# Two buffers for a quarter's output matrices, loaded ahead of its input matrices and transposed one step later

## The chip, the cores and the metric

The kernel runs on one core of a Trainium2 chip. The metric is device time in microseconds (us), and the profile is one execution of the program, recorded by the hardware. Engines are named as the profile does: PE (TensorE matmul), PEld (its weight load), DVE (VectorE), ACT (ScalarE), POOL (GpSimd) and SP (SyncE, which here only issues DMAs). SPq and ACTq are the DMA issues of SP and ACT.

## The reference, cut to what matters

One layer of a decoder trunk, sequence 1024, model width 1024, all float32. A projection makes the inputs of three branches and 3 x 1024 gate logits; the branches are merged under the gates; an output projection, a norm, a SwiGLU block and a second norm follow.

```python
u_s5, x_lru, g_lru, q, k, v, fg, gate_logits = split(x @ w_in)
y_s5  = _s5_branch(u_s5, ...)      # state space, 32 groups x 16 channels, 64 complex states
y_lru = _rglru_branch(x_lru, ...)  # gated linear recurrence, 4 blocks of 128 channels
y_fox = _fox_branch(q, k, v, ...)  # attention with a forget bias, 8 heads
proj  = einsum('blkc,kcd->blkd', stack([y_s5, y_lru, y_fox]), w_branch)
mixed = sum(sigmoid(gate_logits + b_gate) * proj) @ w_out
...
# inside _s5_branch, c = output matrices, b = input matrices of a group
bu = einsum('blgc,gpc->blgp', u, b_bar)
h  = linear_scan(lam_bar, bu)
y  = einsum('blgp,gcp->blgc', h, c).real + d_skip * u
```

## The kernel before, in words

Matmuls reach float32 accuracy in three passes: each operand is split into a high part (ACT casts, `split` at L143) and a low part (DVE subtracts, L129), and `mm3` multiplies high by high, high by low, and low by high. All matmuls of one helper bear L117 in the profile; weights are `wh` and `wl`, activations are two tiles that bear the same letter (`x`, `m` or `s`). A 128 x 512 output from 8 row blocks is 24 matmuls.

Up to the second norm's weights the program is written by three generators that are run against each other: `fox` (attention), `others` (the projection column blocks, `zblock`, 48 matmuls each, and then the merges) and `side` (state space, then the recurrence). Each `yield` adds a number to its generator's clock, and the one with the lowest clock is advanced next; this gives the program order. A scheduler then orders the instructions of each engine by a timeline of its own, with that order as priority, and the result is a fixed, in-order list for each engine. So a number in a `yield` can move instructions on every engine.

`side` first yields 90, then runs `quarter(qd)` for four quarters of 8 groups each (every yield of it times T_S5 = 1.44), then `channel_gate`, then `recurrence` (times T_LRU = 1.246), whose four blocks b = 0 to 3 each do this: a depthwise convolution on DVE; a gate product `ta` and an input product `tx` of 6 matmuls each on PE; tanh on ACT (L844, L845); a reciprocal on DVE (L850); products on POOL; a scan on DVE (L856); a last product on DVE, and a store to `ylru_d` (L859).

`others`, after its last gate block, fetches the four state space outputs and runs `merge(0)`, 16 outputs of 12 matmuls, with L137 on DVE taking each from PSUM; then it fetches the four recurrence outputs back from `ylru_d` (L503) and runs `merge(1)`.

A quarter loads two pairs of input matrices (`b0`, `b1`, L674 and L675) and two natural-layout tiles `nat` of output matrices (L679), transposes each `nat` on PE (L681) and scales it on DVE into `c0` or `c1`. `nat` has one buffer, so the load of the second waits for the transpose of the first. POOL then makes `bb`, `bbs` and the powers `bbp` from the input matrices, and one step later the powers `cl` from the output matrices.

Of the kernel before, what the change touches and what calls it, by code (L numbers as in the profile page):

```python
# [21 lines left out]
P = 128  # L22
# [10 lines left out]
GROUPS, STATES, GCH = 32, 64, 16  # L33
# [24 lines left out]
def trunk(ctx: ExitStack, tc: tile.TileContext, A: dict, out: bass.AP):  # L58
    nc = tc.nc
    PE, ACT, DVE, POOL, SP = nc.tensor, nc.scalar, nc.vector, nc.gpsimd, nc.sync  # L60
# [26 lines left out]
    def name(n):  # L87
        count[0] += 1
        return f"{n}{count[0]}"
# [14 lines left out]
    def few(tag, shape, bufs, pool):  # L104
        return pools[pool].tile(list(shape), F32, name=name(tag), tag=tag, bufs=bufs)
# [4 lines left out]
    def bank(shape=(P, 512), tag="b"):  # L110
        return psum.tile(list(shape), F32, name=name(tag), tag=tag, bufs=3)
# [19 lines left out]
    def ts(e, o, a, s1, op1, s2=None, op2=None):  # L131
        if op2 is None:
            return e.tensor_scalar(o, a, s1, None, op1)
        return e.tensor_scalar(o, a, s1, s2, op1, op2)
# [309 lines left out]
    first_k = done["k"]  # L444


    rows = few("nat", [124, P], 1, "side")

    def put_rows(r, ap, c=slice(0, P)):
        SP.dma_start(rows[r : r + ap.shape[0], c], ap)  # L450
# [213 lines left out]
    c_v = [A["s5_c_re"], A["s5_c_im"]]  # L664
    late_pool = [None]

    def quarter(qd):
        g8 = slice(8 * qd, 8 * qd + 8)
        prm = new("s", shape=(P, 8, 8, GCH))
        b0, b1, c0, c1, bb, bbs = [prm[:, i] for i in range(6)]  # L670
        halves = (slice(0, 64), slice(64, P))
        for i in range(2):
            src = b_v[i][g8].rearrange("g p c -> p g c")
            SP.dma_start(b0[halves[i]], src)  # L674
            SP.dma_start(b1[halves[1 - i]], src)  # L675
        for i, dst in enumerate((c0, c1)):
            nat = few("nat", [P, 2, STATES], 1, "side")
            for e in range(2):
                SP.dma_start(nat[:, e], c_v[e ^ i].rearrange("g c p -> (g c) p")[qd * P : (qd + 1) * P, :])  # L679
            pc = bank([P, 8, GCH])  # L680
            PE.transpose(pc.rearrange("p g c -> p (g c)"), nat.rearrange("p e s -> p (e s)"), ident)  # L681
            ts(DVE, dst, pc, sign, ALU.mult, 1.0 if i == 0 else -1.0, ALU.mult)
# [54 lines left out]
        with after(late_pool[0]):  # L737
            POOL.memset(cc[:, :, 0:1], 1.0)
            POOL.memset(ss[:, :, 0:1], 0.0)
            for i in range(7):  # L740
                n = 1 << i
                e = [t[:, 1 + i, g8].unsqueeze(2).broadcast_to([P, 8, n]) for t in (ctab, stab)]
# [6 lines left out]
        for i in range(2):  # L749
            c = slice(4 * i, 4 * i + 4)  # L750
# [20 lines left out]
        for i in range(2):  # L771
            py = bank([P, 4, P])
            for j in range(4):
                g = 4 * i + j
# [87 lines left out]
    def side():  # L862
        yield T_SIDE
        for qd in range(NB):
            for t in quarter(qd):
                yield T_S5 * t
        yield from channel_gate()
        done["s5"] = True
        for t in recurrence():
            yield T_LRU * t  # L870
        done["lru"] = True
# [277 lines left out]
    for hb in range(NH):  # L1149
        g, more = G[hb], hb + 1 < NH  # L1150
# [199 lines left out]
```

## Time and profile before

| | us |
|---|---|
| median of 3 runs (range) | 1650.58 (1650.56 to 1651.05) |
| the profiled execution's own time | 1650.19 |
| its span, first to last instruction | 1648.4 |
| PE busy in the span | 1592.8 |
| DVE, ACT, POOL busy | 1011.6, 634.5, 599.5 |

The profiled execution's time is its span and 1.8 us around it. PE is busy for 97% of the span, so what can be had or lost is read from PE's idle time, and from the clock that it was granted. A profile row of the timeline names start, duration, engine, line, operation, output and inputs, and in brackets how long the engine was idle before it and what released it.

### The profile page before, as it was taken

What the parts mean: (1) busy time and instruction counts of PE and PEld (TensorE: products, weight loads), DVE (VectorE), ACT (ScalarE), POOL (GpSimd) and SP (SyncE); (2) the same over time, 40 slices, a digit from 0 to 9 for tenths busy, and PEclk for the clock granted to TensorE, in tenths of its full rate; (3) what the DMA queues carried; (4) which work ended last, traced back from release to release, by engine and by line L of the source; (5) the groups of instructions that cost most, each with busy time, mean ns of one, the idle gap of its engine ahead of it and who ended that gap; (6) DMA issues with size and microseconds to landing.
All of it is one profiled execution on the core that took longest, in us unless ns stands there. A gap on an engine that the chain in (4) does not pass through costs nothing.

```text
span 1648.4 us, 20516 instructions
## 1 busy us (share of the span) xinstructions
PE 1592.8 (97%) x7482; PEld 1321.1 (80%) x7482; DVE 1011.6 (61%) x1602; ACT 634.5 (38%) x960; POOL 599.5 (36%) x529
## 2 busy tenths in 40 slices
PE   8989999999899999999999998999999999999997
PEld 6877888877787888888888886788888888778886
DVE  4756575723643467887657769666555555547766
ACT  4425454524633445564213224223222222244442
POOL 0111316333143011112040028599987888400004
PEclk9999999999999999999999998999999999999999
DMA  5343324333332333344754712356544455597752
GB/s 169 76 102 80 80 78 105 77 79 100 88 83 67 116 116 113 114 144 169 246 185 162 244 49 77 126 193 200 171 166 166 154 177 170 202 331 233 245 174 102
DMA packets 219968, 236.09 MB, mean 143 GB/s; under 512 B 33376, under 2 KB 162524, under 8 KB 219868
## 3 DMA queue, kind: packets, MB, share of 16 engines
q1 hardware_dynamic: 192604, 202.83, 39.5%
q10 hardware_dynamic: 27264, 31.96, 5.9%
q8 instruction: 59, 0.97, 0.2%
q14 instruction: 41, 0.34, 0.1%
HBM read 163.96 MB, written 70.78 MB: 142 GB/s over the span
## 4 chain that ended last, share of the span: by engine, by line
PE 78%; DVE 9%; issue 4%; DMA 3%; ACT 3%; POOL 2%; SPq 1%; ACTq 0%; DVEq 0%; POOLq 0%
PE b L117 35%; PE p L117 32%; PE a L117 8%; PE s L117 2%; PE a L341 1%; DMA ws<-w_ffn_down 1%; POOL s L129 1%; DVE r L129 1%; DVE s L129 1%; DVE x L137 1%; DVE wo L129 1%; DMA nck<-ck_d 1%; DVE m L129 1%; DVE x L129 1%; ACT r L1237 1%
## 5 line engine op out<-in xcount | busy, mean ns | idle before, releaser
L117 PE MATMUL b<-x,wh 128*128 128x512 f32 x912 | 351.9, 397 | 2.3 <-ACT s L708 1.7
L117 PE MATMUL b<-x,wl 128*128 128x512 f32 x832 | 328.5, 395 | 0.0
L117 PE MATMUL b<-m,wh 128*128 128x512 f32 x784 | 309.1, 394 | 0.0
L117 PE MATMUL p<-mx,w 128*128 128x512 f32 x1056 | 250.0, 392 | 2.1 <-DVE mx L129 1.3
L117 PEld LDWEIGHTS p<-mx,w 128*128 128x128 f32 x1056 | 199.7, 189 | 44.4 <-issue 1.7
L117 PEld LDWEIGHTS b<-x,wh 128*128 128x128 f32 x912 | 172.9, 190 | 37.4 <-ACT s L708 2.0
L117 PEld LDWEIGHTS b<-x,wl 128*128 128x128 f32 x832 | 157.4, 189 | 31.7
L129 DVE TENSOR_TENSOR x<-x,p 128x512 f32<-128x512 f32 x163 | 108.4, 683 | 109.4 <-PE p L117 92.5
L117 PEld LDWEIGHTS b<-m,wh 128*128 128x128 f32 x784 | 148.8, 190 | 28.7 <-issue 0.2
L117 PE MATMUL p<-w,w 128*128 128x512 f32 x528 | 157.4, 390 | 1.1 <-DVE w L129 1.0
L129 POOL TENSOR_TENSOR s<-s,s 128x1024 f32<-128x1024 f32 (+9 forms) x76 | 77.2, 1015 | 207.4 <-ACT s L852 75.2
L129 DVE TENSOR_TENSOR w<-ws,w 128x1024 fp32r<-128x1024 f32 x88 | 116.0, 1324 | 51.8 <-ACT w L143 51.6
L143 ACT CAST w<-ws 128x1024 fp32r<-128x1024 f32 x88 | 92.1, 1050 | 103.4 <-PE p L117 64.0
L117 PE MATMUL p<-wo,w 128*128 128x512 f32 x528 | 127.3, 389 | 0.0
L129 DVE TENSOR_TENSOR wl<-ws,wh 128x1024 fp32r<-128x1024 f32 x62 | 85.8, 1383 | 65.5 <-ACT wh L143 62.2
L117 PEld LDWEIGHTS p<-w,w 128*128 128x128 f32 x528 | 98.8, 188 | 22.9 <-DVE w L129 2.6
L117 PEld LDWEIGHTS p<-wo,w 128*128 128x128 f32 x528 | 99.1, 188 | 20.5
L143 ACT CAST wh<-ws 128x1024 fp32r<-128x1024 f32 x62 | 65.1, 1050 | 125.0 <-PE b L117 99.2
L129 DVE TENSOR_TENSOR w<-m,w 128x1024 fp32r<-128x1024 f32 x44 | 69.0, 1567 | 63.2 <-ACT w L143 63.2
L129 POOL TENSOR_TENSOR ln<-x,x 128x512 f32<-128x512 f32 x44 | 75.7, 1727 | 63.6 <-ACT x L1172 52.2
L117 PE MATMUL p<-w 128*128 128x512 f32 x264 | 97.5, 390 | 1.1 <-ACT w L143 1.1
L129 POOL TENSOR_TENSOR r<-r,row 128x1024 f32<-128x1024 f32 x7 | 16.7, 2391 | 189.5 <-DVE r L129 184.3
(276 smaller groups left out, 2721.6 us busy)
## 6 DMA issues: line engine op xcount, KB each, us to landing
ws<-w_in SPq DMA_DIRECT2D x48, 512.0 KB, 4.1
ws<-w_ffn_gate SPq DMA_DIRECT2D x27, 512.0 KB, 4.2
gate_d<-zs ACTq DMA_DIRECT2D x48, 256.0 KB, 2.0
zs<-gate_d SPq DMA_DIRECT2D x48, 256.0 KB, 2.8
ws<-w_ffn_up SPq DMA_DIRECT2D x22, 512.0 KB, 4.6
x<-w_ffn_down SPq DMA_DIRECT2D x22, 512.0 KB, 5.6
hid_d<-ln SPq DMA_DIRECT2D x22, 512.0 KB, 3.9
wts_d<-x SPq DMA_DIRECT2D x22, 512.0 KB, 2.6
```

The costliest lines, as they stand in the source:

```text
L117: PE.matmul(o, a, b, start=first, stop=last)
L129: return pin(e.tensor_tensor(o, a, b, op))
L137: return DVE.scalar_tensor_tensor(out=o, in0=a, scalar=s, in1=b, op0=op0, op1=op1)
L143: pin(ACT.copy(hi, src))
L341: PE.transpose(ta[:, j, e, :], pts[e][:, (k0 + j) * P : (k0 + j + 1) * P], ident)
L1237: pin(ACT.activation(r, r, AF.Identity, bias=nm, scale=rs))
```

## The change

The `nat` tag gets two buffers. A quarter issues its four `nat` loads ahead of its four input-matrix loads, yields 5.0 (7.2 on the clock of `side`), and only then transposes. The later steps of a quarter, the channel gate and the recurrence come that much later on the clock of `side`, 28.8 after four quarters.

```diff
--- before.py
+++ after.py
@@ -444,7 +444,7 @@
     first_k = done["k"]
 
 
-    rows = few("nat", [124, P], 1, "side")
+    rows = few("nat", [124, P], 2, "side")
 
     def put_rows(r, ap, c=slice(0, P)):
         SP.dma_start(rows[r : r + ap.shape[0], c], ap)
@@ -669,14 +669,17 @@
         prm = new("s", shape=(P, 8, 8, GCH))
         b0, b1, c0, c1, bb, bbs = [prm[:, i] for i in range(6)]
         halves = (slice(0, 64), slice(64, P))
+        nats = [few("nat", [P, 2, STATES], 2, "side") for _ in range(2)]
+        for i, nat in enumerate(nats):
+            for e in range(2):
+                SP.dma_start(nat[:, e], c_v[e ^ i].rearrange("g c p -> (g c) p")[qd * P : (qd + 1) * P, :])
         for i in range(2):
             src = b_v[i][g8].rearrange("g p c -> p g c")
             SP.dma_start(b0[halves[i]], src)
             SP.dma_start(b1[halves[1 - i]], src)
+        yield 5.0
         for i, dst in enumerate((c0, c1)):
-            nat = few("nat", [P, 2, STATES], 1, "side")
-            for e in range(2):
-                SP.dma_start(nat[:, e], c_v[e ^ i].rearrange("g c p -> (g c) p")[qd * P : (qd + 1) * P, :])
+            nat = nats[i]
             pc = bank([P, 8, GCH])
             PE.transpose(pc.rearrange("p g c -> p (g c)"), nat.rearrange("p e s -> p (e s)"), ident)
             ts(DVE, dst, pc, sign, ALU.mult, 1.0 if i == 0 else -1.0, ALU.mult)
```

**SP's list.** Names are tiles with their numbers; `nat` tiles are the output matrices, `ws` the weights of the projection. Before, at the third quarter, with the next quarter's first tile behind it:

```order
L679 DMA nat688_3519<-s5_c_im 128x64
L679 DMA nat688_3519<-s5_c_re 128x64
L172 DMA ws776_4009<-w_in 128x8x128
L679 DMA nat877_4458<-s5_c_re 128x64
L679 DMA nat877_4458<-s5_c_im 128x64
L172 DMA ws819_4208<-w_in 128x8x128
```

Changed, the third quarter's loads:

```order
L675 DMA nat698_3643<-s5_c_re 128x64
L172 DMA ws665_3323<-w_in 128x8x128
L675 DMA nat698_3643<-s5_c_im 128x64
L675 DMA nat699_3644<-s5_c_im 128x64
L675 DMA nat699_3644<-s5_c_re 128x64
L302 DMA nck568_2815<-ck_d_92 128x8x128
L734 DMA s619_3017<-u_d_522 16x8x128 x8
```

The second tile's loads now follow the first tile's, with no transpose between them, and stand ahead of the quarter's input matrices, which come some ten rows later.

**DVE's list between recurrence block 2 and merge(0).** `s` tiles are the recurrence's, `x` tiles with a `ws` input are the low parts of the state space outputs, `wl` the low parts of the branch weights that merge(0) begins with. Before, from the scan of block 2 on:

```order
L856 SCALAR_TENSOR_TENSOR s1297_6706<-s1306_6739,s1301_6716 128x1024
L129 TENSOR_TENSOR s1297_6706<-s1297_6706,s1296_6703 128x1024
L129 TENSOR_TENSOR s1332_6946<-s1323_6878,s1331_6945 128x1024
L137 SCALAR_TENSOR_TENSOR x1342_6979<-ws1340_6976,x1341_6978 128x1024
L137 SCALAR_TENSOR_TENSOR x1345_6985<-ws1343_6982,x1344_6984 128x1024
L137 SCALAR_TENSOR_TENSOR x1348_6991<-ws1346_6988,x1347_6990 128x1024
L137 SCALAR_TENSOR_TENSOR x1351_6997<-ws1349_6994,x1350_6996 128x1024
L129 TENSOR_TENSOR wl1354_7003<-ws1352_7000,wh1353_7002 128x1024
L129 TENSOR_TENSOR wl1357_7009<-ws1355_7006,wh1356_7008 128x1024
```

Changed, from the reciprocal of block 2 on:

```order
L853 RECIPROCAL s1320_6863<-s1320_6863 128x1024
L137 SCALAR_TENSOR_TENSOR x1330_6939<-ws1328_6936,x1329_6938 128x1024
L137 SCALAR_TENSOR_TENSOR x1333_6945<-ws1331_6942,x1332_6944 128x1024
L134 TENSOR_SCALAR s1358_7042<-s1356_7038,cols91_518 128x1024
L137 SCALAR_TENSOR_TENSOR x1336_6951<-ws1334_6948,x1335_6950 128x1024
L134 TENSOR_SCALAR s1320_6863<-s1320_6863 128x1024
L137 SCALAR_TENSOR_TENSOR s1358_7042<-s1356_7038,cols91_518,s1358_7042 128x1021
L859 SCALAR_TENSOR_TENSOR s1311_6830<-s1320_6863,s1315_6840 128x1024
L137 SCALAR_TENSOR_TENSOR x1339_6957<-ws1337_6954,x1338_6956 128x1024
L137 SCALAR_TENSOR_TENSOR s1358_7042<-s1356_7038,cols91_518,s1358_7042 128x1022
L129 TENSOR_TENSOR s1311_6830<-s1311_6830,s1310_6827 128x1024
L129 TENSOR_TENSOR wl1342_6963<-ws1340_6960,wh1341_6962 128x1024
```

The scan and last product of block 2 stood ahead of all four low parts; now the four stand among them, and the first `wl` of merge(0) stands behind the last product of block 2. On PE's list the last `ta` matmul of block 2 was 156 matmuls ahead of the first one of merge(0) (the 6 of `tx`, three gate blocks of 48, and the 6 `ta` matmuls of block 3); now it is 54 ahead (the 6 of `tx` and one gate block). The first 12 matmuls of merge(0) now all use high parts of weights; the 13th is the first that uses `wl1342`.

**DVE's list between recurrence block 3 and merge(1).** `m` rows take an output of merge(0) from the PSUM tile named last; `wl1418` is the low part of merge(1)'s first weights. Before, around the scan of block 3:

```order
L134 TENSOR_SCALAR s1339_6973<-s1339_6973 128x1024
L137 SCALAR_TENSOR_TENSOR m1371_7092<-zs1372_7093,b1373_7095 128x512
L856 SCALAR_TENSOR_TENSOR s1323_6878<-s1339_6973,s1334_6950 128x1024
L129 TENSOR_TENSOR s1409_7305<-ws1407_7302,s1408_7304 128x1024
L137 SCALAR_TENSOR_TENSOR m1371_7092<-zs1374_7109,a1375_7111 128x512
L129 TENSOR_TENSOR s1323_6878<-s1323_6878,s1322_6875 128x1024
L129 TENSOR_TENSOR s1412_7311<-ws1410_7308,s1411_7310 128x1024
```

Changed:

```order
L137 SCALAR_TENSOR_TENSOR m1389_7189<-zs1390_7190,b1391_7192 128x512
L134 TENSOR_SCALAR s1380_7147<-s1380_7147 128x1024
L137 SCALAR_TENSOR_TENSOR m1389_7189<-zs1392_7206,a1393_7208 128x512
L859 SCALAR_TENSOR_TENSOR s1358_7042<-s1380_7147,s1370_7091 128x1024
L129 TENSOR_TENSOR s1358_7042<-s1358_7042,s1357_7039 128x1024
L129 TENSOR_TENSOR s1412_7311<-ws1410_7308,s1411_7310 128x1024
L137 SCALAR_TENSOR_TENSOR m1394_7230<-zs1395_7231,b1396_7233 128x512
L137 SCALAR_TENSOR_TENSOR m1394_7230<-zs1397_7247,a1398_7249 128x512
L137 SCALAR_TENSOR_TENSOR m1399_7263<-zs1400_7264,b1401_7266 128x512
L137 SCALAR_TENSOR_TENSOR m1399_7263<-zs1402_7280,a1403_7282 128x512
L129 TENSOR_TENSOR s1415_7317<-ws1413_7314,s1414_7316 128x1024
L129 TENSOR_TENSOR wl1418_7323<-ws1416_7320,wh1417_7322 128x1024
```

The scan of block 3 stood behind the output in `b1373`, whose last matmul is 132 ahead of the first of merge(1); now it stands behind the output in `a1393`, whose last matmul is 48 ahead of merge(1). The three instructions that follow on ACT's list are as before: the store of block 3, the cast of its reloaded output, and the cast of merge(1)'s first weights, `wh1417`. On SP the reload and then the loads of those weights follow in this order too.

## Rows read from the trace of the kernel before

**Rows 1.** The page, busy time of each engine in us, its share, instructions.

```profile
PE 1592.8 (97%) x7482; PEld 1321.1 (80%) x7482; DVE 1011.6 (61%) x1602; ACT 634.5 (38%) x960; POOL 599.5 (36%) x529
```

**Rows 2.** Waits of PE: us in total, times, longest.

```profile
PE b L681 <- DMA nat<-s_c_re: 5.1, 3, 2.5
PE a L341 <- DVE pt L133: 3.9, 2, 3.4
```

**Rows 3.** Timeline of PE at the transposes of the third and fourth quarter.

```profile
354.44 0.28 PE L681 MATMUL b<-ident,nat 128*128 128x128 f32 x1
357.06 0.45 PE L681 MATMUL b<-ident,nat 128*128 128x128 f32 x1 [2.35 <-DMA nat<-s_c_re]
...
453.97 0.45 PE L681 MATMUL b<-ident,nat 128*128 128x128 f32 x1 [2.50 <-DMA nat<-s_c_re]
```

**Rows 4.** Timeline of SP: start, duration of the issue.

```profile
355.14 0.42 SPq L679 DMA_DIRECT2D nat<-s_c_re  x1
...
793.97 0.32 SPq L503 DMA_DIRECT2D ws<-ylru_d  x1
794.72 0.93 SPq L172 DMA_DIRECT2D ws<-w_branch  x2
```

**Rows 5.** Stretches behind those transposes; the last three columns: granted clock, DMA share, GB/s.

```profile
357.00:359.00 2.00, 1.95 (x5) 1.60 (x6) 1.96 (x3) 0.00 (x0) 0.00 (x0) 0.50 0.00 0
359.00:361.00 2.00, 2.00 (x8) 1.60 (x7) 0.82 (x2) 0.00 (x0) 1.07 (x1) 0.70 0.83 211
456.00:458.00 2.00, 2.00 (x6) 1.58 (x5) 1.29 (x2) 0.76 (x2) 2.00 (x2) 0.50 0.32 53
458.00:460.00 2.00, 2.00 (x8) 1.57 (x7) 0.00 (x0) 0.00 (x0) 1.92 (x1) 0.70 0.35 99
```

**Rows 6.** Timeline of PE from recurrence block 2 to merge(1).

```profile
730.04 2.58 PE L117 MATMUL b<-s,s 128*128 128x512 f32 x10 [0.53 <-DVE s L129]
...
761.72 0.39 PE L117 MATMUL b<-x,wh 128*128 128x512 f32 x1
...
764.89 0.39 PE L117 MATMUL b<-x,wl 128*128 128x512 f32 x1
...
766.48 1.07 PE L117 MATMUL a<-x,wh 128*128 128x512 f32 x4
...
811.36 0.62 PE L117 MATMUL b<-s,wh 128*128 128x512 f32 x2
```

**Rows 7.** Timeline of DVE from the reciprocal of block 2 to merge(1).

```profile
735.56 6.54 DVE L850 RECIPROCAL s<-s 128x1024 f32<-128x1024 f32 x1
742.03 0.71 DVE L134 TENSOR_SCALAR s<-s,cols 128x1024 f32<-128x1024 f32 x1
742.78 3.31 DVE L137 SCALAR_TENSOR_TENSOR s<-s,cols,s 128x1021 f32<-128x1021 f32 x1
...
750.13 2.28 DVE L856 TENSOR_TENSOR_SCAN s<-s,s 128x1024 f32<-128x1024 f32 x1
752.44 2.36 DVE L129 TENSOR_TENSOR s<-s,s 128x1024 f32<-128x1024 f32 x2
757.23 1.23 DVE L137 SCALAR_TENSOR_TENSOR x<-ws,x 128x1024 fp32r<-128x1024 f32 x1 [2.42 <-ACT x L508]
...
766.52 1.22 DVE L129 TENSOR_TENSOR wl<-ws,wh 128x1024 fp32r<-128x1024 f32 x1
...
789.71 1.22 DVE L129 TENSOR_TENSOR s<-s,s 128x1024 f32<-128x1024 f32 x1
```

**Rows 8.** Timeline of ACT in the same stretch.

```profile
732.56 1.23 ACT L845 ACTIVATE s<-s,c 128x1024 f32<-128x1024 f32 x1
...
790.97 0.33 ACTq L859 DMA_DIRECT2D ylru_d<-s  x1
799.53 1.05 ACT L143 CAST s<-ws 128x1024 fp32r<-128x1024 f32 x1 [8.90 <-DMA ws<-ylru_d]
801.06 1.05 ACT L143 CAST wh<-ws 128x1024 fp32r<-128x1024 f32 x1 [0.48 <-DMA ws<-w_branch]
```

## The prediction

> **What bounds the kernel now.** Read the page first: PE is busy for 97% of the span [rows 1], so 55.6 us (1648.4 - 1592.8) are idle, and everything else hides under PE. Then the list of whom PE waits for. The transposes of `nat` wait for their own load, 5.1 us in three times, against 3.9 for the attention transposes that wait for DVE [rows 2]. The timeline shows why: at 354.44 the first `nat` of the third quarter is transposed, SP then issues the second tile's load at 355.14, and PE stands until 357.06 [rows 3, 4]. One buffer makes this a round trip. In the fourth quarter the same costs 2.50 us before 453.97; the third case is the remaining 0.25.
>
> An idle PE costs more than the idle time. Behind the stall of 2.35 us the granted clock is 0.50 from 357 to 359 and 0.70 from 359 to 361 [rows 5], which loses 1.0 + 0.6 = 1.6 us of PE. Behind the other it is still 0.50 at 456 to 458 and 0.70 to 460 [rows 5], up to 2.6 us counted from 454, but an earlier stall (the 3.4 of rows 2) already stood a few us ahead, so part of this stays.
>
> Second, the far end of `side`. Recurrence and merges meet in the stretch from 730 to 811. PE runs through it with hardly a pause: matmuls start 0.2264 us apart (3.17 us for 14 of them, 761.72 to 764.89), block 2's matmuls restart at 730.04, merge(0) begins at 766.48 and merge(1) at 811.36 [rows 6]. This works since PE had enough other matmuls in between. Here the change is decided.
>
> **The change part by part.**
>
> *The second buffer and the earlier load.* The load no longer waits for a transpose, and a step lies between load and transpose. I take away all three waits: 5.1 us. With them goes the low clock behind the first long one, 1.6 us, and behind the second one something from 0 to 2.6, of which I take half, 1.3. Together -8.0 us, bounds -6.7 and -9.3.
>
> *The order on SP.* Four `nat` issues (0.42 us each or less, [rows 4]) now precede the four loads of input matrices, so these come 1.7 us later at most. POOL's first products wait for them, and they too belong to the step that moved. POOL is busy for 36% of the span [rows 1], and the quarter's transposes of `bbp` are a step further on; I cost it at nothing. Without that cover it is 1.7 us in each quarter, 6.8.
>
> *The step of 5.0, inside the quarters.* Two transposes, two scalings on DVE and nine POOL operations per quarter move; their number and size stay. PE's work is the same. The order of PE, DVE, ACT and POOL from some 100 us on is new, so the attention's waits on DVE and ACT fall elsewhere. The row of 3.9 us [rows 2] stands for their size: one or two such waits can vanish or appear. I take 0 and keep 5 us both ways.
>
> *The step, at the head of merge(0).* This is the first new wait. DVE's list now puts the low part `wl1342` of merge(0)'s first weights behind the tail of recurrence block 2, and PE's list leaves 54 matmuls where 156 were. Follow block 2 from the end of its last `ta` matmul. Before, four of the ten matmuls from 730.04 are `ta`, so it ends near 731.0 [rows 6]. L845 ends at 733.8 (732.56 + 1.23, [rows 8]): 2.8 us. The reciprocal ends at 742.1 [rows 7]: 8.3 more, 11.1. In the new list six DVE operations follow up to the scan: three low parts and one convolution step of about 1.23 each and two scalings of 0.71 [rows 7], less about 0.1 for each overlap: 6.2. The scan takes 2.2 of its 2.28, and low part, convolution step, last product and `wl1342` about 1.2 each, 4.8 [rows 7]. Sum: 11.1 + 6.2 + 2.2 + 4.8 = 24.3 us. One of these steps took 3.31 instead of 1.23 in this stretch before [rows 7], which would make it 26.4. I take 25.0. PE has 54 matmuls and the 12 that need high parts only, 66 x 0.2264 = 14.9 us. So PE waits 10.1 us, bounds 9.4 and 11.5. The low clock falls mostly inside this wait if it comes in two parts (the high parts are late too, as their loads queue behind the state space outputs in three `ws` buffers): nothing more; if it is one wait, 1.6 more. I take 10.1.
>
> What hid this before: behind block 2 stood three gate blocks and the `ta` of block 3, 156 x 0.2264 = 35.3 us, against the same chain.
>
> *The step, at the head of merge(1).* The second new wait. The scan of block 3 now queues on DVE behind the output in `a1393`, and PE can't have finished that until 48 matmuls, 10.9 us, ahead of merge(1). From there: that row on DVE 0.6 (half of a 1.23), scan 2.2, last product 1.2, together 4.0. Then the tail as measured: the product ends at 790.93 (789.71 + 1.22, [rows 7]); the store is issued at 790.97 [rows 8], the reload at 793.97 and the weights at 794.72 [rows 4], the reload is cast at 799.53 and the weights `wh` from 801.06 to 802.11 [rows 8], so 11.2 us from product to weights. 4.0 + 11.2 - 10.9 = 4.3 us of wait. If the weights land as fast as the reload (5.6 us from issue to cast instead of 6.3), 3.5; with one DVE step stretched, 5.5. This wait is as long as the ones of rows 3, so the clock falls behind it: 1.6 us by [rows 5]. Together 5.9, bounds 3.5 (no clock) and 7.1. Before, the weights were cast by 802.1 and PE came at 811.36: 9.3 us to spare [rows 6, 8]. Who waits behind: merge(1)'s DVE and POOL rows, all behind PE. Late next is nothing: from merge(1) on PE's list is the old one, but for the order of its first outputs.
>
> **Sum**, against the profiled execution's own time: 1650.2 - 8.0 + 10.1 + 5.9 = 1658.2 us. That execution is 0.4 under the median of the runs shown, so I say 1658. The likeliest case's own range: gains of 6.7 to 9.3 against losses of 12.9 to 20.2 (11.5 + 1.6 + 7.1), and 5 either way for the attention: 1649 to 1669 if all ends fell together, 1650 to 1666 as I give it.
>
> **The rivals.**
>
> *The change does what it is written to do, and no more: faster.* Then 1650.2 - 8.0 = 1642. For it speaks that PE's waits on `nat` are the largest single entry that the change can reach, and that DVE has idle time (61% busy). The Trainium skill (Trainium Kernel Development and Optimization, Best Practices) says to double-buffer so that loads overlap compute, and by that rule alone the time would be this 1642. The trace agrees with it on the 5.1 us at `nat`, but it shows the further price where the stream ends. It decides if block 2's chain takes no more than 15 us from `ta` to `wl1342`; before, it took 22.7 to the last product alone (731.0 to half of the pair from 752.44, [rows 6, 7]). Chance 0.13.
>
> *Only one new wait: about the same.* If store, reload and weights of block 3 take 7 us instead of 11.2, merge(1) finds its weights. 1650.2 - 8.0 + 10.1 = 1652.3. Against it: two transfers and a cast in sequence stand in those 11.2, and each was measured. With a kind draw in the attention this also is where losses and gains cancel. Chance 0.12.
>
> *Worse in the attention.* The third quarter's first products now stand among attention pieces with no gate matmuls between, the kind of place where PE waited for the 3.9 us of rows 2 before. One more such wait with its clock, 3.4 + 1.6 = 5 us: 1663. Chance 0.15.
>
> **How the numbers follow.** The forecast has 0.60. A measurement of this kernel can tell about 0.2%, 3.3 us, from no change. Faster by more: 0.13, the first rival. Within: 0.12, the second. Slower: 0.75, the forecast and the third. The range leaves out the first rival and the far end of the third: 1648 to 1667.
>
> **What would show it.** Right: no DMA wait at the transposes (L684 then); a wait of PE of about 10 us, in one or two parts, for high and low parts of weights (ACT, DVE) just ahead of 770; another of about 4 us at the first matmul of merge(1), for `wh`, and a clock of 0.5 behind it. From then on the same distances as before. Wrong: PE goes through both heads without a pause, which would mean that the chain of a recurrence block shrank, or that PE comes later to the gate block ahead of merge(0), having lost that time somewhere earlier. The size is wrong if PE's idle time between 100 and 560 us, without `nat`, moves by more than 5 us.

## The result, and the profile after

The changed kernel takes 1669.8 us in the median of six runs (1666.5 to 1671.4), against 1650.8 for the kernel before beside it: a ratio of 1.011, 95% interval 1.0096 to 1.0124. It is slower, as forecast, but by 19 us instead of 8, and the time lies outside the forecast range of 1648 to 1667. The profiled execution took 1668.4 us, 18.2 more than that of before.

The page, PE's row, answers to [rows 1]: 96% of a longer span.

```profile
PE 1598.2 (96%) x7482; PEld 1326.3 (80%) x7482; DVE 1012.7 (61%) x1602; ACT 637.1 (38%) x962; POOL 608.6 (37%) x529
```

Whom PE waits for in the changed kernel (us in total, times, longest). The waits for `nat` of [rows 2] are gone, and L684, where the transposes now stand, is in no row. In their place are two waits for `wh`, one of 3.5 for `tr` and one of 3.7 for `q`.

```profile
PE b L117 <- ACT wh L143: 14.2, 2, 8.4
...
PE a L117 <- DVE tr L129: 4.6, 3, 3.5
PE p L117 <- DVE mx L129: 3.8, 1, 3.8
PE b L117 <- DVE q L129: 3.7, 1, 3.7
```

The timeline of the changed kernel at merge(0), four engines in order of time; it answers to [rows 6, 7].

```profile
748.16 2.88 PE L117 MATMUL b<-s,s 128*128 128x512 f32 x12
754.00 6.55 DVE L853 RECIPROCAL s<-s 128x1024 f32<-128x1024 f32 x1
760.46 4.45 DVE L137 SCALAR_TENSOR_TENSOR x<-ws,x 128x1024 fp32r<-128x1024 f32 x2
764.94 2.24 SPq L172 DMA_DIRECT2D ws<-w_branch  x2
769.27 1.04 ACT L143 CAST wh<-ws 128x1024 fp32r<-128x1024 f32 x1 [2.88 <-DMA ws<-w_branch]
770.37 1.22 PE L117 MATMUL b<-x,wh 128*128 128x512 f32 x2 [8.44 <-ACT wh L143]
...
772.24 1.06 PE L117 MATMUL b<-x,wh 128*128 128x512 f32 x2
773.10 1.05 PE L117 MATMUL a<-x,wh 128*128 128x512 f32 x2
...
774.13 1.22 DVE L129 TENSOR_TENSOR wl<-ws,wh 128x1024 fp32r<-128x1024 f32 x1
775.66 0.47 PE L117 MATMUL b<-x,wl 128*128 128x512 f32 x1
```

Read it upwards from PE. PE stands 8.44 us until `wh` is cast. The cast waits for the load of the branch weights, and SP issues that load at 764.94, right when DVE is done with two low parts of the state space outputs (760.46 + 4.45 = 764.91). The second of them frees a `ws` buffer for the load, and both stood behind the reciprocal of recurrence block 2. The last two rows show a second thing: `wl`, behind the tail of block 2 in DVE's list, ends at 775.35, and the 13th matmul of merge(0), the first that uses it, starts at 775.66, when 12 matmuls of high parts are through. So the high parts, with a low clock behind them, and the low part end together.

The same at merge(1); it answers to [rows 4, 6 to 8].

```profile
809.78 0.69 DVE L134 TENSOR_SCALAR s<-s 128x1024 f32<-128x1024 f32 x1 [0.51 <-POOL s L129]
811.04 0.69 DVE L137 SCALAR_TENSOR_TENSOR m<-zs,a 128x512 f32<-128x512 f32 x1 [0.57 <-DMA zs<-gate_d]
811.65 2.29 DVE L859 TENSOR_TENSOR_SCAN s<-s,s 128x1024 f32<-128x1024 f32 x1
813.97 1.23 DVE L129 TENSOR_TENSOR s<-s,s 128x1024 f32<-128x1024 f32 x1
815.23 0.33 ACTq L862 DMA_DIRECT2D ylru_d<-s  x1
816.84 0.68 DVE L137 SCALAR_TENSOR_TENSOR m<-zs,a 128x512 f32<-128x512 f32 x1
817.55 0.32 SPq L531 DMA_DIRECT2D zs<-gate_d  x1
817.96 0.38 SPq L503 DMA_DIRECT2D ws<-ylru_d  x1
818.40 0.97 SPq L172 DMA_DIRECT2D ws<-w_branch  x2
824.08 1.04 ACT L143 CAST wh<-ws 128x1024 fp32r<-128x1024 f32 x1 [0.61 <-DMA ws<-w_branch]
825.17 1.22 PE L117 MATMUL b<-s,wh 128*128 128x512 f32 x2 [5.74 <-ACT wh L143]
```

Ahead of the reload (L503) and the weights (L172) SP still has loads of gates (L531) to issue. The last goes out at 817.55, when DVE's output row has ended (816.84 + 0.68 = 817.52) and its `zs` buffer is free. The store of block 3, issued at 815.23, lands at 817.8, so here too two things end together, and this trace alone does not tell which of them made the reload late.

To see where the 18.2 us arise I added up, for each execution, the time from each of PE's 7482 matmul starts to the next beyond what that shape takes when nothing stops it (0.226 us for 128x512; taken for each shape and line over all profiled executions). What remains is PE's lost time, waits and low clock together, and does not depend on the order. By stretch of PE's work, in us:

```
                start  quarters  merge(0)  merge(1)  behind
                       (to 760)   head      head
before            7.8     43.3      -0.1      -0.1     15.7
changed           7.5     40.3      11.2       8.4     17.5
difference       -0.3     -3.0     +11.3      +8.5     +1.8
```

In the quarters a gain is left, but 3.0 instead of the 8.0 forecast, and both heads cost more than the 10.1 and 5.9.

### The profile page after: what moved, and what is told of

Its sections match the earlier page's. It is cut to its first block, busy times and chain, and to the rows that moved or that the text cites. A ratio compares the mean times of both kernels' runs of the same rounds, so it can differ in the third digit from the quotient of the medians.

```text
span 1666.7 us, 20520 instructions
## 1 busy us (share of the span) xinstructions
PE 1598.2 (96%) x7482; PEld 1326.3 (80%) x7482; DVE 1012.7 (61%) x1602; ACT 637.1 (38%) x962; POOL 608.6 (37%) x529
## 4 chain that ended last, share of the span: by engine, by line
PE 71%; DVE 6%; DMA 4%; ACT 2%; issue 2%; POOL 1%; SPq 0%; ACTq 0%; DVEq 0%; POOLq 0%
PE p L117 33%; PE b L117 28%; PE a L117 7%; PE s L117 1%; DMA ws<-w_ffn_down 1%; PE a L341 1%; DVE r L129 1%; DVE s L129 1%; DVE x L137 1%; DMA ws<-w_branch 1%; DMA nck<-ck_d 1%; ACT r L1240 1%; DVE x L129 0%; DMA row<-ln_b 0%; POOL s L129 0%
## 5 line engine op out<-in xcount | busy, mean ns | idle before, releaser
L129 POOL TENSOR_TENSOR s<-s,s 128x1024 f32<-128x1024 f32 (+9 forms) x76 | 81.0, 1066 | 182.3 <-ACT s L855 70.4
```

Source lines behind the costliest of these rows:

```text
L129: return pin(e.tensor_tensor(o, a, b, op))
```

## The experiments

Ratios are to the kernel before on the same chip, with 95% intervals. The last columns are PE's lost time in the stretches of the table above.

```
                                   median  ratio   interval         quarters m(0) m(1) behind
1  step alone                      1672.8  1.0132  1.0113 to 1.0151   48.2   11.1  9.1  13.8
2  no step                         1639.8  0.9927  0.9914 to 0.9939   29.8   -0.1 -0.1  17.8
3  step paid back                  1647.4  0.9974  0.9964 to 0.9985   35.4   -0.1 -0.1  18.9
4  recurrence's pace               1655.4  1.0025  1.0016 to 1.0034   41.0    4.5 -0.1  17.8
5  side starts earlier             1655.6  1.0021  1.0011 to 1.0030   42.6   -0.1 -0.1  18.9
6  second buffer alone             1640.2  0.9923  0.9908 to 0.9939   29.3   -0.1 -0.1  18.7
7  merge(0)'s weights first        1665.1  1.0074  1.0058 to 1.0090   41.0    2.0 11.3  18.3
8  no round trip                   1668.5  1.0093  1.0077 to 1.0109   40.7   11.0  5.8  18.4
9  both heads' queues              1652.4  1.0007  0.9998 to 1.0016   40.8    2.0 -0.1  17.6
10 copy on POOL                    1663.7  1.0072  1.0060 to 1.0085   34.7   11.3  9.1  17.7
11 no step, copy on POOL           1640.3  0.9931  0.9919 to 0.9944   30.1   -0.1 -0.1  18.1
12 step of 1.0                     1649.6  0.9991  0.9982 to 1.0001   41.1   -0.1 -0.1  16.3
13 copy on POOL, another bank      1660.8  1.0053  1.0037 to 1.0069   32.3   11.0 10.3  18.2
14 all of 9 and 13                 1644.0  0.9954  0.9939 to 0.9969   32.3    2.0  0.3  18.5
```

### Which part of the change

**1, step alone**, against the kernel before:

```diff
+        yield 5.0
         for i, dst in enumerate((c0, c1)):
             nat = few("nat", [P, 2, STATES], 1, "side")
```

> The kernel before with the step of 5.0 ahead of the transposes alone: one buffer, loads where they were. Theory (the loss comes from the 28.8 that the step adds to the clock of side, paid at the heads of the two merges): PE's list around both merges is that of the changed kernel (54 matmuls between block 2's last ta and merge(0)), so about 8 us of wait at merge(0), 6 at merge(1), and the waits of 5 us for nat stay: 1650.8 + 11.3 + 8.5 + 1.8 + 4.6 = 1677, between 1671 and 1680, slower than the changed kernel. Rival (the loss comes from the two buffers and the early loads, which fill SP's queue and delay weights): 1651 to 1655, no wait for wh at the merges.

**2, no step**, against the changed kernel:

```diff
-        yield 5.0
         for i, dst in enumerate((c0, c1)):
             nat = nats[i]
```

> The changed kernel without the step of 5.0: two buffers and early loads alone. Theory: the list around both merges is that of before (156 matmuls), so no wait for wh there; the waits for nat are 0 to 2 us; 1650.8 - 8 = 1643, with the draw of the attention 1640 to 1647. Rival (loads and buffers cost): about 1669. Third possibility (the load lands too late when the transpose is in the same step): the waits for nat stay and the time is 1649 to 1652.

**6, second buffer alone**, against the kernel before:

```diff
-            nat = few("nat", [P, 2, STATES], 1, "side")
+            nat = few("nat", [P, 2, STATES], 2, "side")
```

(and 2 for 1 where the tag is first used).

> The kernel before with two buffers for nat and nothing else: the second tile's loads are still issued behind the first transpose in the program's text, but no longer wait for it. Theory one (the buffer is what the transposes waited for): the waits for nat are gone, and the time is that of two buffers and early loads without the step, 1637 to 1643. Theory two (the loads must also be issued ahead of the input matrices): the waits for nat stay above 3 us, 1646 to 1651.

Whom PE waits for, step alone and then no step:

```profile
PE b L117 <- ACT wh L143: 15.4, 2, 8.3
...
PE b L682 <- DMA nat<-s_c_re: 4.0, 3, 1.7
```

```profile
PE b L986 <- issue: 5.8, 1, 5.8
PE a L190 <- DMA s<-x: 5.7, 2, 4.6
PE b L117 <- ACT s L779: 4.0, 1, 4.0
```

The step alone brings both waits for `wh` and leaves the waits for `nat`; without it both kinds are gone, and the kernel is 0.7% faster than before. The second buffer alone gives the same 1640, so the early loads bring nothing that can be told: the buffer was what the transposes waited for. The rival that loads and buffers cost is out.

### Is it the clock of side?

**3, step paid back**, against the changed kernel:

```diff
             powers(bbp, bb, bbs, 8, ALU.subtract)
-        yield 8.0
+        yield 3.0
```

> The changed kernel with 3.0 for 8.0 in the quarter's next yield, so that the transposes stay a step later and everything behind them has its old clock. Theory: no wait for wh at the merges (156 matmuls again), no wait for nat; 1643, and since the transposes' place is the only thing new against the kernel without the step, within 4 us of that one. Rival (turning them later is what costs, through the products and powers that lie behind them): near 1669 or at least 5 us above the kernel without the step.

**4, recurrence's pace**: `T_LRU = 1.006` for 1.246. **5, side starts earlier**: `T_SIDE = 61.2` for 90.0. **12, step of 1.0**: `yield 1.0` for 5.0.

> The changed kernel with T_LRU 1.006 for 1.246, so that the recurrence starts 28.8 later but ends at its old clock; the quarters, the attention and the channel gate are those of the changed kernel. 108 matmuls stand between block 2's last ta and the first of merge(0), 24.5 us against a chain of 25. Theory: the waits for wh shrink from 8.4 and 5.7 to 0 to 2 together, the early part keeps the balance of the changed kernel (3.4 better than before): 1647 to 1651. Rival (the waits at the heads come from the loads of weights themselves, not from the distance): 1665 to 1670. If it is 1643 or less, the early part is better than the traces say.

> The changed kernel with 61.2 for the 90 that side yields first: all of side starts 28.8 earlier, so that its end comes at the old clock. PE's list has 156 matmuls again between block 2's last ta and merge(0). Theory (the heads of the merges pay for the clock of side): no wait for wh, 1640 to 1650, where the spread is the new order of the quarters among the attention. Rival (the heads pay for something else that the changed kernel does): at least 1660.

> The changed kernel with a step of 1.0 for 5.0, 5.8 instead of 28.8 on the clock of side at its end. PE's list has 156 matmuls at merge(0). Theory (a step costs at the heads only from the point where the distance no longer covers the chain, and in the quarters whatever the new order of DVE and POOL gives, without proportion to its size): no wait for wh, 1637 to 1650. Rival (each unit of step costs its share of the 30 us between 5.0 and none): 1646, with part of it at the heads.

Wherever PE's list has 156 matmuls again between block 2 and merge(0) (3, 5, 12), both heads lose nothing. At 108 (4) merge(0) loses 4.5, of which 2.4 are these waits, and merge(1) nothing:

```profile
PE b L117 <- DVE wl L129: 1.6, 1, 1.6
...
PE a L117 <- ACT wh L143: 0.8, 1, 0.8
```

The rest of the 4.5 is a third wait, 1.15 for a low part of block 3 whose gate product stands just ahead, and some 0.3 around each of the three; the granted clock is 1.00 throughout. So with the loads as they stand the heads pay for the distance: merge(0) loses 11.2 at 54 matmuls, 4.5 at 108 and nothing at 156. But three of the four times miss. Kernel 3 is 7.6 above the kernel without the step, where its rival said 5 or more: turning later goes with a cost in the quarters (35.4 against 29.8), not at the heads. Kernel 5 is 6 over its range, with 42.6 in the quarters and 4.4 more than before at the start. Kernel 4 is 4 over, about half of it at merge(0) and half behind. Kernel 12 reaches the end of its range, again by the quarters (41.1). With two buffers and little else done but moving `side` against the attention (2 to 6 and 12), that column runs from 29 to 43 us. What I had taken as 0 with 5 either way is the largest unknown of this change.

### What the heads wait for

**7, merge(0)'s weights first**, against the changed kernel (`merge` takes them as an argument):

```diff
+        first = wcols(A["w_branch"][0], 0, 2 * P, NB)
         for b in range(NB):
             fetch(0, b)
-        for _ in merge(0):
+        for _ in merge(0, first=first):
```

> The changed kernel with merge(0)'s first weights loaded ahead of the four state space outputs. Theory (the head of merge(0) waits for DVE, which is in block 2's reciprocal and hands the three ws buffers back late): the wait moves from wh to the outputs' low parts and shrinks by little, from 8.4 to 3 to 7 us in several parts; 1664 to 1668. Rival (the head waits for the weights' load because it is last in the queue): the wait is under 2 us, 1659 to 1661.

**8, no round trip**, against the changed kernel (merge(1) then fetches three outputs only):

```diff
+            if b == NB - 1:
+                Y[1][b] = new("s", F32R), new("s", F32R)
+                split(xc, *Y[1][b])
+            else:
-            ACT.dma_start(ylru_d[b], xc)
+                ACT.dma_start(ylru_d[b], xc)
```

> The changed kernel, in which block 3's output goes to merge(1) straight from its tile, split there, with no store to DRAM and no reload. By the prediction's chain (scan, product, store, reload, weights: 11.2 us from product to weights) the wait of 5.7 us at merge(1) vanishes or falls below 1.5: 1660 to 1663. Rival, from the changed kernel's trace: seven loads of gates stand on SP's list ahead of the reload and the weights, the last of them issued at 817.55 when a zs buffer came free, so the weights are issued no earlier without the reload: the wait stays at 4 to 5.5 us, 1666 to 1669.

**9, both heads' queues**: 7 and 8 together, and merge(1)'s weights loaded in merge(0) at d = 6:

```diff
+        for _ in merge(0, lambda d: first.append(wcols(A["w_branch"][1], 0, 2 * P, NB)) if d == 6 else None, first[0]):
...
+        yield from merge(1, lambda d: fetch(2, d - 2) if 2 <= d < 5 else None, first[1])
```

> The changed kernel with both heads freed of their queues: merge(0)'s first weights are loaded ahead of the state space outputs, merge(1)'s ahead of the last two steps of merge(0) and so ahead of their gates on SP, and block 3's output goes to merge(1) without the round trip. PE's list still has 54 matmuls between block 2's last ta and merge(0). Theory (the heads wait for weights that stand in queues behind things that are late): merge(0) costs 2 as with its weights first, merge(1) 0 to 2, so 1669.8 - 9.3 - 7.5 = 1653, 1650 to 1656. Rival (the short distance itself costs, whatever the loads' order: DVE's chain of blocks 2 and 3 is what is late): 1661 or more, with waits for low parts at the heads.

Kernel 7: merge(0) falls from 11.2 to 2.0, by its rival, though PE's list still has 54 matmuls there. So it was the weights' place that cost, and not the short distance. But the edit does not part the two things that ended together. With the weights loaded and cast early, DVE's list has `wl` ahead of the reciprocal of block 2, and no longer behind its last product:

```profile
751.45 1.23 DVE L129 TENSOR_TENSOR wl<-ws,wh 128x1024 fp32r<-128x1024 f32 x1 [9.65 <-ACT wh L143]
...
756.64 6.55 DVE L854 RECIPROCAL s<-s 128x1024 f32<-128x1024 f32 x1
```

DVE's chain of block 2 is as long as it was; `wl`, on which the prediction built its 10.1, has only left it. Whether early high parts alone, with `wl` in its old place, would have gained anything is not shown; as `wl` ended at 775.35, I estimate 0.3 us (775.66 - 775.35). The time of kernel 7 moves only to 1665.1, since merge(1) then waits 8.6 instead of 5.7: PE comes there 5.6 us earlier (at 813.8 instead of 819.4), and the weights are cast only 2.8 earlier.

Kernel 8: the rival's time again, but only part of its reason. The chain's store and reload are gone, block 3's output is split by 816.1, and the weights are issued at 817.82, 0.6 earlier than in the changed kernel. The six loads of gates ahead of them are out by 817.01; from there SP waits for a `ws` buffer, which DVE frees with the low part of another reloaded output, the first of three from 816.57, at 817.79. PE still waits 4.0 us:

```profile
805.92 11.09 SPq L531 DMA_DIRECT2D zs<-gate_d  x6
817.82 2.64 SPq L172 DMA_DIRECT2D ws<-w_branch  x3
...
814.83 1.23 DVE L129 TENSOR_TENSOR s<-s,s 128x1024 fp32r<-128x1024 f32 x1 [0.52 <-ACT s L143]
...
816.57 3.49 DVE L129 TENSOR_TENSOR s<-ws,s 128x1024 fp32r<-128x1024 f32 x3
...
822.23 1.04 ACT L143 CAST wh<-ws 128x1024 fp32r<-128x1024 f32 x1 [4.58 <-DMA ws<-w_branch]
```

Kernel 9 sets both weights free of their queues, and the 19.6 us of both heads shrink to 1.9 at the same distance of 54 matmuls; 1652.4 was forecast as 1653. That the short distance itself costs is out. From 740 to 850 us PE has one wait left:

```profile
PE b L117 <- DVE wl L129: 1.3, 1, 1.3
```

### What the quarters lose

Two waits of the changed kernel have no partner in [rows 2]. First the one for `tr`:

```profile
318.25 0.68 DVE L129 TENSOR_TENSOR q<-b,q 128x512 fp32r<-128x512 f32 x1
...
319.40 1.09 POOL L303 TENSOR_SCALAR_AFFINE_SELECT ndk<-nck 128x1024 f32<-128x1024 f32 x1 [11.59 <-DMA nck<-ck_d]
...
326.25 0.69 DVE L747 COPY s<-eab 128x1024 f32<-128x1024 f32 x1 [7.32 <-POOL s L129]
327.00 0.68 DVE L129 TENSOR_TENSOR tr<-a,tr 128x512 fp32r<-128x512 f32 x1
327.73 0.86 PE L117 MATMUL a<-tr,q 128*128 128x256 f32 x5 [3.47 <-DVE tr L129]
```

DVE stands 7.3 us at a copy of the quarter's, since POOL still uses the same tile `r8` as its scratch, and the attention's `tr` is next on DVE's list. POOL is late because it stood 11.6 us itself, at a row of the attention (`ndk`) that waited for a load. The Trainium skill (PSUM — Partial Sum Buffer, Engine vs sequencer instructions) says that the queues of VectorE, ScalarE and GpSimdE are strictly first in, first out; these rows agree, with `tr` 0.75 us behind the copy's start. **10, copy on POOL**, against the changed kernel:

```diff
-        DVE.tensor_copy(r8, eab[:, 1, g8].unsqueeze(2).broadcast_to([P, 8, P]))
-        DVE.memset(r8[:, :, 0:1], 0.0)
+        POOL.tensor_copy(r8, eab[:, 1, g8].unsqueeze(2).broadcast_to([P, 8, P]))
+        POOL.memset(r8[:, :, 0:1], 0.0)
```

> The changed kernel with the copy of eab (and the memset behind it) on POOL in place of DVE. In the changed kernel DVE stands 7.3 us at this copy near 319 to 326, since POOL is still writing the same tile, and the attention's low part tr queues behind it; PE waits 3.5 for it and runs at a low clock behind. Theory (DVE waiting in order for POOL is what the attention lost): that wait of PE goes, with its clock 5.2 us: 1664.5, 1662 to 1667. Rival (the wait is then for POOL's longer work, or another of the attention's waits takes its place): 1668 to 1672.

**11**, the same edit without the step:

> Two buffers and early loads without the step (1640), with the copy of eab on POOL. There no wait of PE stands behind this copy, so by the theory it changes nothing that can be told: 1637 to 1643. If POOL's four longer stretches count, 1643 to 1647; below 1636 the copy cost something that the waits don't show.

The wait for `tr` goes (its row falls from 4.6 to 1.0), the time falls by 6.0 to 1663.7, and without the step the same edit changes nothing (1640.3). So the copy costs only where a row that PE needs soon stands behind it. That is a matter of the order, and not of the step alone: the kernel before pays for it too (PE waits 2.4 us for a `tr` behind this copy, shown below), as do kernels 5 and 12 (2.8 and 2.1), and kernel 2 does not, though DVE stands 6.7 us at the copy there.

The second wait, in the changed kernel:

```profile
561.28 0.58 ACT L757 COPY s<-b 64x512 f32<-64x512 f32 x1
...
563.36 1.41 DVE L129 TENSOR_TENSOR q<-b,q 64x512 fp32r<-64x512 f32 x2
564.92 0.77 PE L117 MATMUL b<-x,wh 128*128 128x512 f32 x1 [3.75 <-DVE q L129]
```

PE is at a projection block that needs a PSUM bank. `bank` has three of tag `b`: two hold the fourth quarter's state products, which ACT has begun to copy, and one the last keys, which DVE drains until 564.8. **13, copy on POOL, another bank**, against 10:

```diff
-            st = bank([P, 4, P])
+            st = bank([P, 4, P], "ba"[i] if qd == 3 else "b")
```

> The changed kernel with the copy of eab on POOL and, in the fourth quarter alone, the first of the two state products in a PSUM bank of tag a instead of b. In the changed kernel PE waits 3.7 us before 564.92 until DVE has drained the last key columns (q): the two products and the keys hold all three b banks. Theory (the step brought the fourth quarter's products next to the last keys, and the banks are what PE waits for): with a b bank free the wait goes, with its clock 4.5 us against the kernel with the copy alone: 1663.7 - 4.5 = 1659, 1657 to 1661. Rival (PE waits for DVE anyway, the next reader of the keys or the products): 1663 to 1667.

The edit gives the second of the two products, and not the first as I wrote, the bank of tag `a`. The wait for `q`, 3.1 in kernel 10, is gone, and the time falls by a further 3.0, inside the range though not by the whole 4.5 (the quarters lose 2.4 less). The intervals of 10 and 13 overlap a little, so the size of this step is less certain than the end of the wait. The Trainium skill (Trainium Kernel Development and Optimization, Best Practices) says to mind PSUM pressure, as "TensorE tiling speeds up compute but not PSUM evacuation"; there is no such tiling here, but these rows agree with the second half, with 3.7 us of PE for one bank that was not yet emptied.

**14, all of 9 and 13.**

> The changed kernel with all of it together: both heads freed of their queues (1652.4), the copy of eab on POOL (6.0 less) and the fourth quarter's first state product in a bank of tag a (4.5 less). The step of 5.0 stays. If the four waits are the whole of what the step cost, they add: 1652.4 - 6.0 - 4.5 = 1642, 1639 to 1645, within 5 of the kernel without the step (1640). If something else of the step costs, or one wait takes another's place: 1646 or more.

1644.0: the gains add up (1652.4 - 6.0 - 3.0 = 1643.4). With the step of 5.0 still in, edits elsewhere bring the time to 4 us above the kernel without the step (1639.8), and below the kernel before.

## Why the prediction was wrong, point by point

The prediction had the sign and the place of the loss. It had the quarters, the head of merge(1) and what lies behind at the wrong size. Against the forecast of +8.0 the profile has +18.2.

- **The waits for `nat`, -8.0: without the step too small, and outside its bounds.** Kernels 2 and 6 lose 13.5 and 14.0 less in the quarters than the kernel before. The waits are gone as forecast (5.1); the rest is clock and order. But the terms do not simply add: with the step on both sides, kernel 1 against the changed one, the buffers gain 48.2 - 40.3 = 7.9. The double-buffer rule weighed as a rival there holds for the buffer alone: 1640.2.
- **The step inside the quarters, 0 with 5 either way: the step that failed most.** Between kernel 2 and the changed one it is 40.3 - 29.8 = +10.5. The row of 3.9 us that I took as the size of one such wait was sound; that two of them would come, each with its clock (5.4 us in all for `tr`, 6.8 for `q`), was not allowed for. Kernel 13, which has neither, loses 8.0 less in the quarters than the changed kernel (40.3 - 32.3). One such wait, 5 us with its clock, was the third rival, with 0.15; it stood beside the forecast and not in its sum. With one buffer the step costs only 48.2 - 43.3 = 4.9, so its price too hangs on the order it meets. The cause was in reach: the trace of before shows DVE waiting for POOL at this same copy, 8.5 us in two times, and PE waiting 2.4 for a `tr` behind one of them (the view names the short memset that ends with it). I had counted what the step moves as number and size of instructions, not as places in DVE's list where it waits for POOL. Net, however it is split, `nat` and step gave -3.0 instead of -8.0. The sign that I had set for a wrong size, a move of over 5 us in PE's idle time between 100 and 560 without `nat`, did not show it: 17.0 before and 15.9 changed, since idle time leaves out the low clock and the wait for `q` ends after 560. The rows of before, from the view by line and from the view of waits (after "until" stands what DVE waited for: us, times):

```profile
L744 DVE COPY s<-eab x4: 678/692/696, 209.2 to 521.0; 128x1024 f32<-128x1024 f32 x4
its engine sat idle before it (us, times) until:
  POOL s L129: 8.5, 2
...
PE a L117 <- DVE s L745: 2.4, 1, 2.4
```

- **The head of merge(0), 10.1: size nearly right, mechanism half of it.** It lost 11.3, a wait of 8.4 and 2.9 of clock, inside the bounds of 9.4 and 11.5. The chain was well costed: `wl` ends at 775.4, 25.8 us behind block 2's last `ta` (749.5), against 25.0 (part of that is luck: its six operations ahead of the scan add up to 5.7 from the rows quoted, not 6.2, and one of them took 3.4 us). But PE stood for the high parts, which the prediction mentions only in passing. They came late in the queue of `ws` buffers, and with the low clock behind them ended 0.3 us after `wl`. Kernel 7 takes both away, and with them 9.2 of the 11.2.
- **The head of merge(1), 5.9: 8.5 measured.** DVE took 6.65 us instead of 4.0 from the end of the output in `a1393` (PE's last 48 matmuls end at 819.4, so 808.55) to the product's end (815.20): a scaling that waits for POOL stands ahead of that output, and its gates come 0.57 late. From product to weights it was 9.9 instead of 11.2. So 6.65 + 9.9 - 10.9 = 5.65, measured 5.74, and 2.7 of clock where I had 1.6. Of the tail, store and reload alone counted for 1.7 of the 5.7 (kernel 8); the rest goes when the weights are loaded ahead of the gates and of the reloads' `ws` buffers as well (kernel 9).
- **"Late next is nothing": +1.8.** The wait for `mx` is 3.8 instead of 1.3, with the same list on PE. In all other kernels with two buffers it is 2.0 to 3.9, with the step and without; kernel 1, with one buffer and the step, has none. So it does not go with the step; whether it goes with the second buffer is open, as no experiment was on it.

The sum of errors is -5.5 + 10.5 + 1.2 + 2.6 + 1.8, and -0.3 at the start: 10.3. Four of the five have one sign, and the range had no room for that.

What stays open: what else the quarters lose, 32.3 in kernel 14 against 29.8 in kernel 2, and why a step of 1.0 (kernel 12) costs them 11.3 by other waits than the step of 5.0. I only know that one of its waits is again for a `tr` behind the copy (2.1 us), that the others are for other rows and no longer, and that the clock is at 0.50 for some 10 us from 650 on. How much of the 11.2 at merge(0) was for the high parts alone and how much for `wl` stays open too.

## What to carry to other kernels

A second buffer and a later consumer are two changes: here the buffer alone gave the whole gain, and the delay was paid at the stream's far end and wherever in-order engines of two streams meet. Before you cost a step that moves, list each instruction in it that waits for another engine in the trace of before, and ask what will stand behind it in its new place. Where a head waits, look at what its load queues behind (buffers, other loads on SP) as well as at the arithmetic chain, since both may end together. And where a redraw of the order is one term, take its spread from several kernels (here 13 us), not from one row.

## What the runs showed of the hardware

The low clock lasts well past the end of a wait. Windows of 2 us in the changed kernel at merge(0), and at the waits for `tr` and, in the last row, for `q`; the third column from the end is the granted clock.

```profile
766.00:768.00 2.00, 0.00 (x0) 0.00 (x0) 2.00 (x3) 0.40 (x1) 0.00 (x0) 0.50 0.82 246
772.00:774.00 2.00, 2.00 (x7) 1.52 (x6) 2.00 (x2) 0.35 (x1) 0.00 (x0) 0.50 0.48 118
776.00:778.00 2.00, 2.00 (x10) 1.66 (x9) 1.96 (x3) 1.06 (x1) 0.00 (x0) 1.00 0.87 285
```

```profile
326.00:328.00 2.00, 0.27 (x2) 0.27 (x3) 1.70 (x5) 0.00 (x0) 0.22 (x1) 1.00 0.00 0
328.00:330.00 2.00, 2.00 (x12) 1.81 (x12) 1.44 (x4) 0.85 (x2) 0.00 (x0) 0.67 0.03 8
330.00:332.00 2.00, 2.00 (x6) 1.55 (x5) 0.59 (x1) 0.00 (x0) 0.00 (x0) 0.50 0.79 198
...
568.00:570.00 2.00, 2.00 (x6) 1.57 (x5) 2.00 (x4) 0.00 (x0) 0.00 (x0) 0.50 0.00 0
```

A clock of 1.00 is 2.4 GHz, 0.50 is 1.2. Behind a wait of 8.4 us PE still ran at 0.50 for some 5 us (0.43 from one matmul to the next, as 772.24 and 773.10 with two each show above, instead of 0.23); behind one of 3.5 the clock fell only when PE was already at work. The price was 2.9 us behind 8.4, 2.7 behind 5.7, 3.0 behind the 3.7 for `q`, and about 1.7 behind the 3.5 for `tr`: it does not follow the length of the wait. At merge(0) it would not all come back, since `wl` was not ready earlier. I had priced it at 1.6 where I counted it, from the stalls of 2.4 us in [rows 5].
